# RWKV's three projections: both weight chunks split ahead, then all matmuls in one row

## The chip, the cores and the metric

The kernel runs on one core of one Trainium2 chip. The metric is device time in microseconds (us) of one launch. A core has a matrix engine (PE, with weight loads shown apart as PEld), a vector engine (DVE), a scalar engine (ACT), GpSimd (POOL) and SyncE (SP), which here issues the DMA transfers. Each engine runs its own instructions strictly in the order in which they stand in its program, and semaphores make it wait for others. PE's clock is granted by a throttle at one of two levels, 1.2 and 2.4 GHz; the profile shows a mean of them as a share of full speed.

## The reference

The function is a two-layer decoder trunk on x of 512 tokens by 1024 columns, all in fp32. In each layer two token mixers run on the same normalized input and are merged by gates; a feed-forward part and a small per-layer embedding part follow.

```
h   = rmsnorm(x)
q, k, v, rw, gate_a, gate_b = split(h @ w_in)
y_att = sliding_window_attention(rope(q), rope(k), v, sinks) @ w_o_att
y_rw  = rwkv7_time_mix(rw, ...) @ w_o_rw
x += rmsnorm((sigmoid(gate_a)*y_att + sigmoid(gate_b)*y_rw) @ w_out)
x += rmsnorm((gelu(conv(h2 @ w_up)[a]) * conv(h2 @ w_up)[b]) @ w_down)
x += rmsnorm(sigmoid(x @ w_ple_gate) * (p @ w_ple))
```

The change lies in rwkv7_time_mix. It takes r, k and v (1024 columns each, 16 heads of 64) from h, shifts each by one token, forms a decay from a low-rank product and runs a recurrence over the tokens, in which each head has a 64 x 64 state:

```
r, k, v = shifted(h @ w_r), shifted(h @ w_k), shifted(h @ w_v)
state = state*w_t + (state @ a_t) b_t^T + v_t k_t^T
y_t   = state @ r_t
```

The kernel computes the recurrence in eight chunks of 64 tokens, which needs for each chunk the products of the decayed a, r, b and k (the tiles AR, bk, A and AM) and the inverse of a unit triangular matrix (the tile Z).

## The kernel before, in words

**Matmuls in two parts.** A product in fp32 is made of three fp32r matmuls: the weight tile w (128 columns, 4 blocks of 128 rows, 256 KB) is loaded by one DMA on SP; ACT writes its rounded part wh (L125, called in load_w); DVE subtracts and writes the rest wl (L155). mm3 (L244 to L249) then issues three matmuls of 512 columns for each block of 128 rows: wh by the high part of the activations (L247), wh by their low part (L248), wl by the high part (L249). A projection of 1024 rows has two such chunks, 24 matmuls. Its chunk loads are called w_r.10 and w_r.11 below for column block j=5 of w_r (chunks 2j and 2j+1). The weight pool has, for class "m", two buffers for w, three for wh and three for wl; the sums stand in a PSUM tile pm (two buffers) or pf (one).

**The RWKV stage.** rwkv_prep (L581) prepares one column block j of 128 columns, which holds two heads; there are eight in a layer. It makes k by a projection and a shift (an ACT instruction and a DVE instruction, L366 to L368), the decay (thw, D, Di), kksq with a matmul of ones and its sums to DRAM (ssp), bk and the a-half of AR, then r by a projection and a shift, the r-half of AR, the 32 small matmuls A of 128 x 128, masked by DVE into AM, bkT by transposes, and v by a projection and a shift. rwkv_group (L737) takes two preparations as one group (four groups in a layer): rwkv_inverse (L674) solves the triangular system by 62 short DVE instructions on Z, stores and reloads Z through DRAM (zd), and finishes it with small matmuls of 32 x 32 on PE (t1 and z12, with ACT and DVE copies between them); then a scan over the eight chunks runs, a chain of matmuls of 64 x 64 (xs, sp) with ACT and DVE copies between them.

**What sets the order.** All is traced into one program, and a scheduler puts every instruction in an order on its engine by its priority, the place at which the program emitted it, and by what it waits for. Work of other parts, above all the projections for the gates (w_gb) and the attention output (w_oa), which stand later in the program, is put between the small matmuls where the scheduler sees an engine waiting. tc.high_priority(offset=60), which the change uses, lifts what is emitted within it by 60 places in that priority. The order is fixed when the program is built; on the chip no engine departs from it.

Of the kernel before, what the change touches and what calls it, by code (L numbers as in the profile page):

```python
# [19 lines left out]
P = 128  # L20
T = 512
DM = 1024
KT = DM // P
# [32 lines left out]
class Trunk:  # L56
# [525 lines left out]
    def rwkv_prep(self, l, j, gi, R, X2, DC, ssp, nd):  # L582
        nc, a, h, vv, dv, rp = self.nc, self.a, self.h, self.vv, self.dv, R.rp
        NP_ = 32
        c1 = slice(j, j + 1)
        Tm = R.T
        q = Ctx()

        def ch(t):
            return t.rearrange("p (c t) -> p c t", t=C)  # L590
        k = self.shift(self.proj(a["w_k"][l, j], h), "k", j, Tm("k"))
        wa2 = self.load_w(a["w_wa2"][l, j], 2, low=((slice(64, 128), slice(0, 1)), (slice(0, 64), slice(1, 2))))
        th, ta = Tm("thw"), Tm("tha")
        for i, (t, n) in enumerate(((th, "w0h"), (ta, "a0h"))):
# [30 lines left out]
            self.tt(bk[:, :, x, :], ch(us[x]), ch(Di), ALU.mult)  # L625
        self.ts(ta, ta, dv["ka1"][:, c1], dv["ka2"][:, c1])
        self.tt(k, k, ta, ALU.mult)
        r = self.shift(self.proj(a["w_r"][l, j], h), "r", j, Tm("r"))
        self.tt(rv, ch(r), ch(D), ALU.mult)
        self.stt(r, r, vv("r_k")[:, c1], k, ALU.mult, ALU.mult)  # L630

# [15 lines left out]
        for hf in range(2):  # L647
# [4 lines left out]
            t = rp.tile([P, 4, P], F32, name="bkT", tag="bkT", bufs=6)  # L652
            self.act(t, tp.rearrange("p (c x) -> p c x", c=4))
            q.bkT.append(t)
        v = self.shift(self.proj(a["w_v"][l, j], h), "v", j, Tm("v"))
        bon = self.PT("bonus")
        self.last_prep = nc.tensor.matmul(bon, self.blockones, r, start=True, stop=True).ins
        vp = self.PT("vT")
# [536 lines left out]
```

## Time and profile before

| | before |
|---|---|
| median of 3 runs | 2365.49 us (2357.16 to 2371.89) |
| the profiled execution | 2361.03 us, span 2359.2 us |
| mean granted PE clock | 0.976 |
| PE busy | 2230.6 us, 95% of the span, 14340 matmuls |
| PE weight loads busy | 1757.7 us, 75% |
| DVE busy | 1555.0 us, 66% |
| ACT busy | 1123.3 us, 48% |
| POOL busy | 26.5 us, 1% |

The profiled execution is 4.46 us below the median of the runs. The RWKV stage of layer 0 lies at about 220 to 640 us of the span, that of layer 1 at about 1385 to 1810 us. An instruction's row gives its start, its duration, its engine and line, its tiles as out<-in, the number of like instructions drawn together (x16), and in brackets how long the engine had been idle before it and what ended that. PE's durations overlap: a 512-column matmul is shown with 0.39 us, and the next starts 0.23 us after it.

### The profile page before, as it was taken

To read this page: it belongs to the slowest core of one execution; us is meant where nothing else is said; L and a number is where in the kernel's file an instruction comes from. 1 tells how busy PE (TensorE), PEld (TensorE's weight loads), DVE (VectorE), ACT (ScalarE), POOL (GpSimd) and SP (SyncE) were. 2 spreads that over 40 slices of the span, in tenths; PEclk is the share of its full clock that TensorE was granted. 3 is DMA by queue.
4 is the path that set the end of the run, shared out by engine and by line. 5 is a ranking of instruction groups with operands and counts; after the bars stand their busy time and mean duration, and the time that the engine had idled before them with its cause. 6 is when DMAs were issued, how large, how long until landed. Compare 5 with 4: busy or idle time off the path is not lost. (4 is left out here: it accounts for less than half of the span.)

```text
span 2359.2 us, 39516 instructions
## 1 busy us (share of the span) xinstructions
PE 2230.6 (95%) x14340; PEld 1757.7 (75%) x14340; DVE 1555.0 (66%) x3683; ACT 1123.3 (48%) x2450; POOL 26.5 (1%) x86
## 2 busy tenths in 40 slices
PE   7899999999999999999898999999999999999995
PEld 6666776667689788888795667766677887888895
DVE  6764589767566777733777647778566668776355
ACT  4466445544444544432445655545444445444332
POOL 1000000000000000000000000000000000000000
PEclk9999999989999999999999999999899999999998
DMA  4522333245571332342334233332356713333422
GB/s 146 163 79 94 108 90 86 79 123 169 176 250 35 123 99 94 94 119 87 99 115 145 88 110 95 90 91 83 107 162 198 239 58 104 98 95 102 121 72 81
DMA packets 206818, 269.39 MB, mean 114 GB/s; under 512 B 72096, under 2 KB 88992, under 8 KB 206624
## 3 DMA queue, kind: packets, MB, share of 16 engines
q1 hardware_dynamic: 206624, 266.88, 37.0%
q8 instruction: 113, 1.85, 0.3%
q14 instruction: 81, 0.66, 0.1%
HBM read 218.95 MB, written 42.47 MB: 111 GB/s over the span
## 5 line engine op out<-in xcount | busy, mean ns | idle before, releaser
L125 ACT ACTIVATE wh<-w 128x512 fp32r<-128x512 f32 (+1 forms) x590 | 353.1, 606 | 556.7 <-PE pm L248 176.8
L155 DVE TENSOR_TENSOR wl<-w,wh 128x512 fp32r<-128x512 f32 (+2 forms) x574 | 376.6, 662 | 263.4 <-ACT wh L125 255.6
L249 PE MATMUL pm<-hh,wl 128*128 128x512 f32 x1040 | 424.0, 408 | 9.4 <-DVE wl L155 9.2
L247 PE MATMUL pm<-hh,wh 128*128 128x512 f32 x1040 | 424.6, 408 | 2.8 <-DVE Z L696 1.1
L248 PE MATMUL pm<-hl,wh 128*128 128x512 f32 x1040 | 420.1, 404 | 0.1
L249 PEld LDWEIGHTS pm<-hh,wl 128*128 128x128 f32 x1040 | 198.0, 190 | 56.5 <-DVE wl L155 12.9
L247 PEld LDWEIGHTS pm<-hh,wh 128*128 128x128 f32 x1040 | 198.0, 190 | 49.4 <-issue 5.6
L247 PE MATMUL pf<-hh,wh 128*128 128x512 f32 x544 | 219.2, 403 | 16.2 <-ACT wh L125 10.4
L248 PEld LDWEIGHTS pm<-hl,wh 128*128 128x128 f32 x1040 | 197.6, 190 | 46.6 <-issue 6.5
L249 PE MATMUL pf<-hh,wl 128*128 128x512 f32 x544 | 216.8, 398 | 3.2 <-DVE wl L155 3.0
L248 PE MATMUL pf<-hl,wh 128*128 128x512 f32 x544 | 215.8, 397 | 0.0
L134 DVE SCALAR_TENSOR_TENSOR cv<-un,vec,cv 128x510 f32<-128x510 f32 (+1 forms) x176 | 131.0, 750 | 24.6 <-ACT cv L125 22.0
L247 PEld LDWEIGHTS pf<-hh,wh 128*128 128x128 f32 x544 | 102.5, 188 | 45.9 <-ACT wh L125 20.3
L249 PEld LDWEIGHTS pf<-hh,wl 128*128 128x128 f32 x544 | 102.4, 188 | 32.6 <-DVE wl L155 8.6
L248 PEld LDWEIGHTS pf<-hl,wh 128*128 128x128 f32 x544 | 102.6, 189 | 21.3 <-issue 1.8
L247 PE MATMUL pm<-uh,wh 128*128 128x512 f32 (+1 forms) x248 | 89.1, 359 | 3.6 <-ACT wh L125 3.6
L249 PE MATMUL pm<-uh,wl 128*128 128x512 f32 (+1 forms) x248 | 89.1, 360 | 0.0
L248 PE MATMUL pm<-ul,wh 128*128 128x512 f32 (+1 forms) x248 | 88.8, 359 | 0.0
L125 ACT ACTIVATE cv<-un,vec 128x512 f32<-128x512 f32 x88 | 71.3, 814 | 25.4 <-DVE un L128 25.4
L128 DVE TENSOR_TENSOR acc<-acc,sq 128x256 f32<-128x256 f32 (+1 forms) x114 | 50.1, 464 | 37.9 <-ACT sq L125 37.2
L530 DVE CUSTOM_DVE_ANT_0 sm<-scores,tmask 128x256 f32<-128x256 f32 (+1 forms) x128 | 43.5, 384 | 36.0 <-PE scores L117 36.0
L128 DVE TENSOR_TENSOR un<-pm,rs 128x512 f32<-128x512 f32 x56 | 38.5, 690 | 41.2 <-PE pm L249 41.1
(402 smaller groups left out, 4457.9 us busy)
## 6 DMA issues: line engine op xcount, KB each, us to landing
w<-in_w_up_dram SPq DMA_DIRECT2D x156, 256.0 KB
w<-in_w_dn_dram SPq DMA_DIRECT2D x80, 256.0 KB
w<-in_w_q_dram SPq DMA_DIRECT2D x32, 256.0 KB
w<-in_w_ga_dram SPq DMA_DIRECT2D x32, 256.0 KB
w<-in_w_k_dram SPq DMA_DIRECT2D x32, 256.0 KB
w<-in_w_r_dram SPq DMA_DIRECT2D x32, 256.0 KB
w<-in_w_v_dram SPq DMA_DIRECT2D x32, 256.0 KB
w<-in_w_gb_dram SPq DMA_DIRECT2D x32, 256.0 KB
```

What stands on the lines that cost most here:

```text
L125: return self.nc.scalar.activation(out=out, in_=in_, func=func, **kw)
L128: return self.nc.vector.tensor_tensor(out=out, in0=in0, in1=in1, op=op)
L134: return self.nc.vector.scalar_tensor_tensor(out=out, in0=in0, scalar=s, in1=in1, op0=op0, op1=op1)
L155: self.nc.vector.tensor_tensor(out=wl, in0=w, in1=wh.bitcast(F32), op=ALU.subtract)
L247: mm(ps, wh, ah, start=start, stop=False)
L248: mm(ps, wh, al, start=False, stop=False)
L249: return mm(ps, wl, ah, start=False, stop=stop).ins
L530: nc.vector.tensor_tensor_reduce(out=sm[i][:, par * 256:par * 256 + KW], in0=scs[par][:, x * 256:x * 256 + KW], in1=tm, scale=1.0, scalar= ...
```

## The change

The three calls of proj in rwkv_prep are replaced. proj loads and splits one chunk of four row blocks, issues its 12 matmuls, then does the same for the second chunk. The new function ahead loads and splits both chunks by the existing function whole, within high_priority(offset=60); the new function pr then takes one PSUM tile and issues all 24 matmuls. Loads, splits and matmuls are the same in number and size.

```diff
@@ -588,7 +588,16 @@
-        k = self.shift(self.proj(a["w_k"][l, j], h), "k", j, Tm("k"))
+        def ahead(name):
+            with self.tc.high_priority(offset=60):
+                return self.whole(a[name][l, j], P, "m")
+
+        def pr(ws):
+            ps = self.PM("m")
+            for i, w in enumerate(ws):
+                self.mm3(ps, w, h[i], i == 0, i == KT - 1)
+            return ps
+        k = self.shift(pr(ahead("w_k")), "k", j, Tm("k"))
...
-        r = self.shift(self.proj(a["w_r"][l, j], h), "r", j, Tm("r"))
+        r = self.shift(pr(ahead("w_r")), "r", j, Tm("r"))
...
-        v = self.shift(self.proj(a["w_v"][l, j], h), "v", j, Tm("v"))
+        v = self.shift(pr(ahead("w_v")), "v", j, Tm("v"))
```

In the order of the instructions the column blocks j=0 to 4 of each layer change by a few rows; j=5, 6 and 7 change much, on PE, ACT, DVE and SP. POOL's order stays. Lines below L591 are nine higher in the changed kernel (L715 becomes L724).

**The first place: DVE, column block j=5 of layer 0.** Before, wl_4615 is the first chunk of w_r (k_4563 is this block's k, Z the inverse of the group before, yo a later result of the group before that):

```order
L134 SCALAR_TENSOR_TENSOR AR_4589<-k_4563,nkk_571,D_4583 128x8x63
L696 TENSOR_TENSOR Z_3787<-Z_3787,Z_3788 128x14x5
L128 TENSOR_TENSOR v_4510<-bonus_4513,v_4510 128x512
L694 TENSOR_TENSOR Z_3788<-rin_3789,Z_3787 128x56
L131 TENSOR_SCALAR AR_4589<-k_4563,nkk_571 128x8
L128 TENSOR_TENSOR yo_3315<-yo_3315,bv_3313 128x512
L696 TENSOR_TENSOR Z_3787<-Z_3787,Z_3788 128x14x4
L128 TENSOR_TENSOR yo_3315<-yo_3315,g_3314 128x512
L694 TENSOR_TENSOR Z_3788<-rin_3789,Z_3787 128x45
L128 TENSOR_TENSOR Di_4584<-k_4563,Di_4584 128x512
L696 TENSOR_TENSOR Z_3787<-Z_3787,Z_3788 128x15x3
L155 TENSOR_TENSOR wl_4615<-w_4611,wh_4613 128x512
```

With the change both chunks of w_r (wl_4614 and wl_4620) stand here, ahead of the shift of this block's k:

```order
L128 TENSOR_TENSOR grt_3297<-gry_3295 128x16
L155 TENSOR_TENSOR wl_4614<-w_4610,wh_4612 128x512
L134 SCALAR_TENSOR_TENSOR grt_3297<-grt_3297,gvar_3284 128x16
L703 TENSOR_TENSOR Z_3788<-rin_3789,Z_3787 128x91
L134 SCALAR_TENSOR_TENSOR gry_3295<-grt_3297,gry_3295 128x16
L155 TENSOR_TENSOR wl_4620<-w_4616,wh_4618 128x512
```

The first split of w_r moved ten instructions of Z forward, and the second stands four rows behind it; the shift of k, which stood ahead of both, is now 12 rows behind the second. On SP the two loads of w_v for j=5 moved likewise, ahead of the small transfers of ssp and zd; on PE the 24 matmuls of this block's v moved ahead of its matmuls A.

**The second place: PE, the inverse of the third group (j=4 and 5) of layer 0.** t1 and z12 are the inverse's small matmuls, A those of j=7, pm_5659 the sum of v for j=7, pm_6306 one of w_gb. Before:

```order
L715 MATMUL t1_4837<-zT_4833,AM_4430 32x32
L117 MATMUL A_5617<-AR_5552,bk_5553 128x128
L117 MATMUL A_5618<-AR_5552,bk_5553 128x128
L724 MATMUL z12_4856<-Z_4750,t1_4834 32x32 x8
L117 MATMUL A_5617<-AR_5552,bk_5553 128x128
L724 MATMUL z12_4857<-Z_4750,t1_4834 32x32 x8
L117 MATMUL A_5618<-AR_5552,bk_5553 128x128
```

With the change:

```order
L724 MATMUL t1_4837<-zT_4833,AM_4430 32x32
L247 MATMUL pm_6306<-hh_109,wh_6327 128x512
L248 MATMUL pm_6306<-hl_110,wh_6327 128x512
L733 MATMUL z12_4856<-Z_4750,t1_4834 32x32 x8
L249 MATMUL pm_6306<-hh_109,wl_6329 128x512
L733 MATMUL z12_4857<-Z_4750,t1_4834 32x32 x8
L247 MATMUL pm_6306<-hh_111,wh_6327 128x512
```

The matmuls A of j=7 stand ahead of this inverse now, and 512-column matmuls of w_gb stand between its steps.

**The third place: PE, the inverse of the last group (j=6 and 7) of layer 0.** pf_6622 is a sum of w_oa. Before:

```order
L715 MATMUL t1_5800<-zT_5796,AM_5393 32x32
L247 MATMUL pf_6622<-hh_105,wh_6625 128x512
L248 MATMUL pf_6622<-hl_106,wh_6625 128x512
L724 MATMUL z12_5819<-Z_5713,t1_5797 32x32 x8
L249 MATMUL pf_6622<-hh_105,wl_6627 128x512
L724 MATMUL z12_5820<-Z_5713,t1_5797 32x32 x8
L247 MATMUL pf_6622<-hh_107,wh_6625 128x512
```

With the change:

```order
L724 MATMUL t1_5799<-zT_5796,AM_5392 32x32
L724 MATMUL t1_5800<-zT_5796,AM_5393 32x32
L733 MATMUL z12_5819<-Z_5713,t1_5797 32x32 x8
L733 MATMUL z12_5820<-Z_5713,t1_5797 32x32 x8
L724 MATMUL t1_5848<-zT_5845,AM_5615 32x32
L724 MATMUL t1_5849<-zT_5845,AM_5616 32x32
```

All matmuls of pf_6622 now stand ahead of this inverse, and none is left between its steps and those of the scan's first chunk. In layer 1 the inverse of the last group keeps 512-column matmuls of w_oa between its steps.

## Rows read from the trace of the kernel before

**Rows 1.** The page's first part: busy time of the engines, share of the span, number of instructions.

```profile
PE 2230.6 (95%) x14340; PEld 1757.7 (75%) x14340; DVE 1555.0 (66%) x3683; ACT 1123.3 (48%) x2450; POOL 26.5 (1%) x86
```

**Rows 2.** The page's costliest groups: line, engine, operation, out<-in, shapes, count, then busy time and mean ns of one, then the idle time of the engine just before them and what ended most of it.

```profile
L125 ACT ACTIVATE wh<-w 128x512 fp32r<-128x512 f32 (+1 forms) x590 | 353.1, 606 | 556.7 <-PE pm L248 176.8
L155 DVE TENSOR_TENSOR wl<-w,wh 128x512 fp32r<-128x512 f32 (+2 forms) x574 | 376.6, 662 | 263.4 <-ACT wh L125 255.6
L249 PE MATMUL pm<-hh,wl 128*128 128x512 f32 x1040 | 424.0, 408 | 9.4 <-DVE wl L155 9.2
L247 PE MATMUL pm<-hh,wh 128*128 128x512 f32 x1040 | 424.6, 408 | 2.8 <-DVE Z L696 1.1
```

**Rows 3.** Stretches of 40 us in the RWKV stage of layer 0: start and end, length, then busy time and number of instructions of PE, PEld, DVE, ACT and POOL, then the granted PE clock, the DMA engines' busy share and GB/s.

```profile
400.00:440.00 40.00, 35.91 (x403) 24.94 (x403) 26.26 (x67) 16.36 (x42) 1.22 (x4) 0.91 0.47 126
440.00:480.00 40.00, 39.23 (x352) 27.75 (x351) 38.08 (x109) 24.71 (x59) 0.53 (x1) 1.00 0.27 80
480.00:520.00 40.00, 36.26 (x356) 26.04 (x354) 21.80 (x52) 16.04 (x38) 1.22 (x4) 0.79 0.39 97
560.00:600.00 40.00, 39.82 (x497) 27.81 (x495) 20.60 (x49) 19.83 (x55) 1.22 (x4) 1.00 0.54 161
```

**Rows 4.** The same view and columns, layer 1.

```profile
1560.00:1600.00 40.00, 35.26 (x354) 24.70 (x352) 25.09 (x62) 17.15 (x39) 1.22 (x4) 0.87 0.38 97
1600.00:1640.00 40.00, 35.69 (x368) 24.53 (x367) 37.80 (x112) 22.52 (x61) 0.53 (x1) 0.96 0.26 81
1640.00:1680.00 40.00, 37.74 (x270) 28.22 (x269) 24.40 (x56) 18.21 (x36) 1.22 (x4) 0.80 0.35 92
1680.00:1720.00 40.00, 39.56 (x438) 27.55 (x438) 27.85 (x83) 20.26 (x59) 0.00 (x0) 0.90 0.43 130
```

**Rows 5.** PE's waits between 380 and 500 us: the waiting group, what it waited for, us in total, how many times, the longest.

```profile
PE pm L249 <- DVE wl L155: 3.6, 3, 1.7
PE A L117 <- DVE AR L128: 2.4, 1, 2.4
PE pm L247 <- DVE Z L696: 1.1, 1, 1.1
PE pm L597 <- ACT thw L125: 0.9, 1, 0.9
```

**Rows 6.** PE's waits between 1545 and 1690 us, the same columns.

```profile
PE A L117 <- DVE AR L128: 3.0, 2, 2.4
PE A L117 <- DVE AM L128: 2.4, 2, 1.9
PE pm L597 <- ACT thw L125: 2.1, 1, 2.1
PE pm L249 <- DVE wl L155: 1.4, 1, 1.4
...
PE pm L247 <- ACT wh L125: 0.6, 1, 0.6
```

**Rows 7.** PE in order of time, the projection of r for j=5 and the matmuls A behind it, layer 0.

```profile
402.12 0.50 PE L249 MATMUL pm<-hh,wl 128*128 128x512 f32 x1 [1.37 <-DVE wl L155]
402.46 0.40 PE L247 MATMUL pm<-hh,wh 128*128 128x512 f32 x1
402.70 0.39 PE L248 MATMUL pm<-hl,wh 128*128 128x512 f32 x1
...
410.16 1.20 PE L117 MATMUL A<-AR,bk 64*128 64x128 f32 x16 [2.38 <-DVE AR L128]
```

**Rows 8.** DVE in order of time in the same stretch: the splits of w_r.10 and w_r.11, and the shift of r.

```profile
401.38 0.68 DVE L155 TENSOR_TENSOR wl<-w,wh 128x512 fp32r<-128x512 f32 x1
...
404.48 0.68 DVE L155 TENSOR_TENSOR wl<-w,wh 128x512 fp32r<-128x512 f32 x1
...
408.54 0.75 DVE L134 SCALAR_TENSOR_TENSOR r<-pm,vec,r 128x511 f32<-128x511 f32 x1 [0.35 <-ACT r L125]
```

**Rows 9.** ACT in order of time: the first chunk of w_v for j=5, layer 0.

```profile
410.76 0.63 ACT L125 ACTIVATE wh<-w 128x512 fp32r<-128x512 f32 x1 [2.25 <-DMA w<-in_w_v_dram]
```

**Rows 10.** Shorter stretches, with the columns of rows 3: the third group's inverse and first scan steps of layer 0, the matmuls A of j=5 in layer 1, the third group's inverse and first scan steps of layer 1.

```profile
500.00:515.00 15.00, 15.00 (x166) 11.29 (x164) 7.13 (x17) 4.63 (x14) 0.00 (x0) 0.55 0.21 55
1580.00:1590.00 10.00, 10.00 (x120) 7.65 (x119) 2.41 (x5) 1.27 (x4) 0.00 (x0) 0.56 0.47 122
1667.00:1688.00 21.00, 20.93 (x193) 15.39 (x189) 7.25 (x20) 4.64 (x14) 0.00 (x0) 0.51 0.15 36
```

**Rows 11.** PE in order of time in the third group's inverse of layer 0.

```profile
501.84 1.06 PE L715 MATMUL t<-zT,AM 32*32 32x32 f32 x32
```

**Rows 12.** PE in order of time in the last group's inverse and first scan step of layer 0.

```profile
571.18 0.69 PE L715 MATMUL t<-zT,AM 32*32 32x32 f32 x32
571.80 0.50 PE L247 MATMUL pf<-hh,wh 128*128 128x512 f32 x1
572.14 0.40 PE L248 MATMUL pf<-hl,wh 128*128 128x512 f32 x1
572.47 0.69 PE L724 MATMUL z<-Z,t 32*32 32x32 f32 x16
...
579.96 0.40 PE L248 MATMUL pf<-hl,wh 128*128 128x512 f32 x1
580.28 0.45 PE L782 MATMUL sp<-X,bkT 128*64 128x64 f32 x8
```

**Rows 13.** DVE in order of time: the last step of that sum of w_oa, with the gate.

```profile
582.95 0.69 DVE L134 SCALAR_TENSOR_TENSOR ta<-ta,pf 128x512 f32<-128x512 f32 x1 [0.38 <-PE pf L249]
```

## The prediction

> **What bounds the kernel now.** I read the totals first. PE is busy for 2230.6 of 2359.2 us [rows 1], no other engine for more than 66%, so a change that only moves work can win two things: idle time of PE, 128.6 us in all, and time in which PE's clock is at the lower level. The groups say who ends PE's idle time where weight splits are concerned: all 1040 matmuls of L249 into pm waited 9.2 us for wl together, those of L247 2.8 us for anything [rows 2]. That is the first thing to see: the waits which the title of the change is about are worth about 9 us in 2361, spread over all parts of the kernel that use pm, not RWKV alone.
>
> The second look is at the stage, cut into stretches of 40 us. In layer 0 PE is short of busy time only where j=5 and j=7 are prepared, 35.91 and 36.26 us of 40, and DVE is nearly full in the stretch between, 38.08 [rows 3]. Layer 1 has the same picture, with 35.26, 35.69 and 37.74 us [rows 4]. The same rows carry the clock: 0.91, 0.79, 0.87, 0.96, 0.80 and 0.90. Its shortfall, (1 - clock) x 40, is 3.6 + 8.4 = 12.0 us in layer 0 and 5.2 + 1.6 + 8.0 + 4.0 = 18.8 us in layer 1. So the slow clock is worth more here than the idle time.
>
> The third look is at the waits by name [rows 5, 6] and, for the clock, at shorter stretches [rows 10]. The slow stretches at 500 and 1667 us have no idle time to speak of, 15.00 of 15.00 and 20.93 of 21.00 us busy, and 0.55 and 0.51 of the clock. What runs in them are the inverse's 32 x 32 products, A and the scan's 64 x 64 products with few 512-column matmuls between. The last group's inverse of layer 0 has the same small products with 512-column matmuls between them [rows 12], in a stretch at clock 1.00 [rows 3]. The same 32 products take 1.06 us in the one [rows 11] and 0.69 in the other [rows 12].
>
> **The change part by part.** Loads, splits and matmuls stay the same in number and size, so no busy time is added. Only order counts, and only j=5, 6 and 7 of each layer change theirs. Splits cost 0.68 us on DVE and wh 0.63 us on ACT [rows 8, 9].
>
> *Column block j=5.* PE waited 1.37 us for wl of w_r.10 and 2.38 us for AR [rows 7]; layer 1 has 1.4 and 2.4 and another 0.6 for wh of w_v, which came late [rows 6]; in layer 0 that load came late too (ACT idle for 2.25 us on it [rows 9]) behind the small transfers on SP. All of these go: the splits of w_r stand earlier, v's loads stand ahead of those transfers, and 23 of v's matmuls, 23 x 0.23 = 5.3 us, now run while r is shifted and AR formed, against the 2.38 us needed. Gone are 3.75 and 4.4 us. What is late next is k: its shift stands behind two splits, 2 x 0.69 = 1.4 us, and the whole chain of D, Di, bk and AR behind it, on a DVE that is 95% full. The cover is r's 24 matmuls; a bound below is nothing, above 2.8 us if v's two splits ahead of bk count as well. I take 1.4, as only the first pair stands ahead of k. Gain 2.35 + 3.0 = 5.35 us (from 1.0 + 1.6 to 3.75 + 4.4).
>
> *j=6.* In layer 0 it had no wait of size, and it now gets its 512-column matmuls of k in a row while two more splits stand ahead of Z's steps on DVE; its next k load stands behind ssp and zd on SP. I charge two waits of the size of the late wh, 0.6 [rows 6], less some cover: 0.9 us (from 0 to 1.4). In layer 1 the waits for AR, 0.6 of the 3.0, and for AM, 2.4 [rows 6], get v and k matmuls as cover; I take half of 3.0, 1.5 (from 0 to 3.0). Together a gain of 0.6 us.
>
> *j=7, waits.* In layer 0 they are 0.9 for thw, 1.1 for Z and 3.6 - 1.37 = 2.2 for wl, of which 1.67 is here: 3.7 us [rows 5]. The thw chain is untouched. The wl wait goes, but v's splits now stand ahead of AM's masks on DVE, and A runs earlier, when less has been done for it. I take 0.9 won (from -1.0 to 3.7). In layer 1 the 2.1 us for thw stay [rows 6]: 0.
>
> *Third group, clock.* A of j=7 now runs before the inverse, and w_gb's 512-column matmuls stand between the inverse's and the scan's steps, the mix that ran at 1.00 in the last group. The shortfall is 0.45 x 15 = 6.8 us in layer 0 and 0.49 x 21 = 10.3 us in layer 1 [rows 10]. The small products wait for copies in part, so not all of it comes back: 6 and 8 us (from 0 to 6.8 and 10.3). At j=5 of layer 1 another 0.44 x 10 = 4.4 us is short [rows 10]; A there stays a block of small products, I take 1 (from 0 to 4.4).
>
> *Last group of layer 0.* Its cover is gone: from 571.80 to 579.96 us 14 matmuls of pf lay in seven places between the steps [rows 12], at 0.33 us from start to start 14 x 0.33 = 4.6 us, which now stand ahead and leave as many us of bare waiting. On DVE the last step of that sum, 0.69 us [rows 13], now stands ahead of the transpose on which the first small product waits. So 5.3 us of idle time, and I expect the clock to fall in or after it, for some 6 us at half, 3 us. Cost 8.3 us (from 4.6 to 12).
>
> The loads' place on SP and wh's on ACT cost nothing by themselves: ACT is 16 to 25 us of 40 busy [rows 3], and if that cover failed the late-load wait of 0.6 us [rows 6] a block would come back.
>
> Sum: 5.35 + 0.6 + 0.9 + 6 + 8 + 1 - 8.3 = 13.6 us won. Of the profiled execution, 2361.0 - 13.6 = 2347.4; the median of the three runs shown is 4.5 higher than that execution, so the forecast is 2365.5 - 13.6 = **2352 us**. With the terms' bounds not all at one end it reaches from 2344 to 2362.
>
> **The page and the row on the clock.** Rows 10 show the low level in stretches without idle time. The Trainium skill, TensorE: Matmul & The Clock Gate, section "HAM oscillation — how this bites in real kernels", puts a falling clock down to waits of PE between bursts of matmuls. By that rule exchanging A for w_gb in a busy stretch returns nothing, the clock terms 6, 8 and 1 are zero, and the last group of layer 0, which does get waits, is the only place where the clock could change. The rows of the slow stretches speak against it, so I keep the terms; it is the third rival.
>
> **Rivals.** *The clock comes back everywhere (chance 0.17).* If the full shortfall of both layers, 12.0 + 18.8 us, went, with 5.35 of waits at j=5, 3.0 - 0.9 = 2.1 at j=6, 0.9 at j=7, and the last group at its 5.3 us of idle time alone: 30.8 + 8.35 - 5.3 = 33.9 us, 2332 us. For it speaks that the stretch at 560 us holds 1.00 with the same small products; against it that A at j=5 keeps its own block.
>
> *Slower: the splits ahead hold up Z (0.17).* At j=5 and 6 DVE is 38.08 and 37.80 us of 40 busy and Z's 62 steps run there one behind another, each behind what is put between. Six splits a block, 6 x 0.69 = 4.1 us, now stand ahead of Z's end, AM and the k chain. It decides once PE's filler, which is finite, has run out before the inverse can start: every us of delay then is a us of PE. The last group of layer 0 shows that point reached. Were it so for j=5 and 6 in both layers, 4 x 4.1 = 16.5 us come in with the 8.3, against 8.2 us of the removed waits at j=5 and no clock won: 16.6 us slower, 2382 us. Against it: the splits were on the same DVE before, only later, and all had to be done by the same matmuls.
>
> *The clock is not a matter of the filler (0.16).* With the clock terms at nothing the waits won are 6.85 and the last group costs 5.3 to 8.3: 1.5 us faster to 1.5 slower, 2364 to 2367 us. For it: 1580 to 1590 us has 10.00 of 10.00 busy and 0.56 [rows 10], so busy time alone does not hold the clock, and I do not know that w_gb does.
>
> The forecast keeps 0.50.
>
> **How the numbers follow.** The range reaches from 2332, the first rival, to 2374, half way to the slower one's time; below and above it about a tenth each is left. A measurement of this kernel can tell about 1% from no change, 24 us: under 2342 or over 2389. Faster by that much are most of the first rival and the forecast's best corner, 0.13 + 0.03 = 0.16; slower the upper end of the second rival, 0.05; the rest, 0.79, is within.
>
> **What would show it.** In the changed profile, PE's waits for wl at j=5 and for AR behind r are gone in both layers; the third group's inverses are at a clock above 0.9 in both layers; the last group of layer 0 shows PE idle for about 5 us between t1, z12 and xs, with the clock falling there; k's shift and thw at j=6 and 7 end PE's new waits, none over 2 us. The forecast is wrong if the third group's stretches stay at half clock with w_gb in them, if PE's idle time before the inverses of both layers grows by more than the 8 us removed at j=5, or if the last group of layer 1 loses its cover as well.

## The result and the profile after

| | before | with the change |
|---|---|---|
| median | 2363.85 us (2357.16 to 2371.89, 4 runs) | 2338.68 us (2334.68 to 2339.89, 4 runs) |
| ratio | | 0.9889, 95% interval 0.9855 to 0.9923 |
| profiled execution | 2361.03 us | 2339.11 us |
| span, mean PE clock | 2359.2 us, 0.976 | 2337.1 us, 0.984 |

The change makes the kernel 25 us faster by the medians, 22.1 us by the spans of the two profiled executions. The forecast was 13.6 us. The ratios here and below are the record's estimates over all runs; they can differ by up to 0.002 from the quotient of the two medians.

The page's first part, to be read against [rows 1]:

```profile
PE 2211.3 (95%) x14340; PEld 1742.5 (75%) x14340; DVE 1550.4 (66%) x3683; ACT 1123.8 (48%) x2450; POOL 27.5 (1%) x86
```

PE has the same 14340 matmuls and is busy 2230.6 - 2211.3 = 19.3 us less. Its idle time fell from 128.6 to 2337.1 - 2211.3 = 125.8 us, by 2.8 us. So seven eighths of what was won are matmuls that run faster, and one eighth is waiting that went. The costliest groups say the same of the waits for splits, against [rows 2]: L249 into pm had waited 9.2 us for wl, and now waits 6.4.

```profile
L247 PE MATMUL pm<-hh,wh 128*128 128x512 f32 x1040 | 425.2, 409 | 2.2 <-ACT wh L125 1.8
L249 PE MATMUL pm<-hh,wl 128*128 128x512 f32 x1040 | 420.7, 404 | 6.4 <-DVE wl L155 6.4
```

The stage in each layer, cut from PE's first small matmul of the first inverse to the last normalization of the merge. The columns are those of [rows 3]. Before:

```profile
342.10:718.40 376.30, 363.10 (x3240) 267.47 (x3239) 262.75 (x662) 186.70 (x441) 4.72 (x14) 0.96 0.48 144
1508.10:1889.90 381.80, 367.16 (x3240) 272.05 (x3239) 263.52 (x662) 186.58 (x441) 4.72 (x14) 0.95 0.47 142
```

With the change:

```profile
342.70:711.10 368.40, 354.98 (x3239) 261.90 (x3238) 260.73 (x662) 187.37 (x441) 4.72 (x14) 0.98 0.48 147
1499.30:1864.30 365.00, 354.06 (x3239) 259.32 (x3238) 261.45 (x662) 186.16 (x441) 4.73 (x14) 1.00 0.49 148
```

Layer 0's stage is 7.9 us shorter, layer 1's 16.8, together 24.7; the remaining 2.6 us were lost outside these cuts, where at most a few rows of the order change. Length less busy time is PE's idle time: 13.2 us before and 13.4 after in layer 0, 14.6 and 10.9 in layer 1. All of layer 0's gain and 13.1 of layer 1's 16.8 us are busy time, with the clock at 0.98 and 1.00 in place of 0.96 and 0.95.

PE's waits between 380 and 500 us, which answer to [rows 5]:

```profile
PE pm L606 <- ACT thw L125: 1.2, 2, 0.8
PE pm L249 <- DVE wl L155: 1.0, 1, 1.0
PE ss L621 <- ACT kksq L125: 0.9, 2, 0.4
PE pm L247 <- ACT wh L125: 0.6, 1, 0.6
```

And between 1545 and 1690 us in layer 1, which answer to [rows 6]:

```profile
PE pm L606 <- ACT thw L125: 2.6, 2, 1.8
PE pm L249 <- DVE wl L155: 1.8, 1, 1.8
PE pm L247 <- ACT wh L125: 1.2, 2, 0.6
```

The waits for AR, 2.4 us in layer 0 and 3.0 in layer 1, are gone, and so is the wl wait of r at j=5. New ones, for thw, kksq and wh, end the places that came next, and in layer 1 a wait of 1.8 us for wl that was not there before, at 1642.59 us.

The slow stretches of [rows 10] and the last group of layer 0, with the columns of [rows 3]: first the third group of layer 0, then its last group, then the third group of layer 1.

```profile
498.00:518.00 20.00, 20.00 (x297) 13.72 (x295) 7.85 (x23) 9.88 (x27) 0.00 (x0) 1.00 0.45 124
564.00:582.00 18.00, 15.20 (x242) 11.31 (x243) 5.75 (x16) 7.31 (x22) 0.00 (x0) 0.62 0.43 138
1656.00:1676.00 20.00, 20.00 (x299) 13.51 (x299) 8.72 (x25) 9.60 (x28) 0.00 (x0) 1.00 0.53 159
```

The third groups, at 0.55 and 0.51 before, are at 1.00. The inverse of the last group of layer 0, at 1.00 before, is the one that got worse. PE there in order of time, to be set against [rows 12]:

```profile
564.27 0.69 PE L724 MATMUL t<-zT,AM 32*32 32x32 f32 x32 [2.10 <-DVE zT L719]
565.40 1.09 PE L733 MATMUL z<-Z,t 32*32 32x32 f32 x32 [0.43 <-ACT t L125]
567.17 0.85 PE L724 MATMUL t<-zT,AM 32*32 32x32 f32 x32 [0.68 <-DVE zT L719]
568.43 1.73 PE L733 MATMUL z<-Z,t 32*32 32x32 f32 x32 [0.41 <-ACT t L125]
...
571.36 0.69 PE L784 MATMUL xs<-scr,Z 64*64 64x64 f32 x8 [0.58 <-ACT scr L125]
572.47 0.69 PE L791 MATMUL sp<-X,bkT 128*64 128x64 f32 x8 [0.42 <-DVE X L786]
```

The gaps add up to 2.10 + 0.43 + 0.68 + 0.41 + 0.58 + 0.42 = 4.6 us, and the same products slow down on the way, t from 0.69 to 0.85 us and z from 1.09 to 1.73.

### The profile page after: what moved, and what is told of

Read it like the earlier page. It is cut to its first block, busy times and chain, and to the rows that moved or that the text cites. A ratio compares the mean times of both kernels' runs of the same rounds, so it can differ in the third digit from the quotient of the medians.

```text
span 2337.1 us, 39500 instructions
## 1 busy us (share of the span) xinstructions
PE 2211.3 (95%) x14340; PEld 1742.5 (75%) x14340; DVE 1550.4 (66%) x3683; ACT 1123.8 (48%) x2450; POOL 27.5 (1%) x86
## 5 line engine op out<-in xcount | busy, mean ns | idle before, releaser
L249 PE MATMUL pm<-hh,wl 128*128 128x512 f32 x1040 | 420.7, 404 | 6.4 <-DVE wl L155 6.4
L249 PEld LDWEIGHTS pm<-hh,wl 128*128 128x128 f32 x1040 | 196.6, 189 | 50.4 <-DVE wl L155 7.9
L249 PE MATMUL pf<-hh,wl 128*128 128x512 f32 x544 | 217.4, 400 | 3.3 <-DVE wl L155 3.1
L247 PEld LDWEIGHTS pf<-hh,wh 128*128 128x128 f32 x544 | 102.8, 189 | 46.2 <-ACT wh L125 18.8
L249 PEld LDWEIGHTS pf<-hh,wl 128*128 128x128 f32 x544 | 102.7, 189 | 32.6 <-DVE wl L155 8.9
L249 PE MATMUL pm<-uh,wl 128*128 128x512 f32 (+1 forms) x248 | 89.1, 360 | 0.0
```

The costliest lines, as they stand in the source:

```text
L247: mm(ps, wh, ah, start=start, stop=False)
L249: return mm(ps, wl, ah, start=False, stop=stop).ins
```

## The experiments

Two theories stood at the start. Mine: the raised priority moves the matmuls so that 512-column matmuls come to lie in the third group's inverse, and this decides the clock there. The rival of the first runs: it is the 24 matmuls in a row, or each projection's early splits bring a share.

**Whole projections without the priority.** The with statement goes, all else stays:

```diff
         def ahead(name):
-            with self.tc.high_priority(offset=60):
-                return self.whole(a[name][l, j], P, "m")
+            return self.whole(a[name][l, j], P, "m")
```

> The loads and splits of both chunks stand together and the 24 matmuls in a row, but without the raised priority. In the order of the instructions the third group's inverse has 4 and 5 512-column matmuls between its steps and 15 and 12 matmuls A, as before the change. Theory (the raised priority carries the gain, by what it moves into the third group): the time of before, 2362 us within 6, third group at clock 0.5 to 0.6. Rival (24 matmuls in a row carry it): the changed kernel's time, 2339 us.

Measured: 2358.15 us against 2358.48 before, ratio 0.9994 (0.9979 to 1.001). The third groups stay slow:

```profile
498.00:514.00 16.00, 16.00 (x183) 12.24 (x179) 7.67 (x19) 4.78 (x14) 0.00 (x0) 0.57 0.27 72
1663.00:1681.00 18.00, 17.93 (x159) 12.81 (x160) 7.15 (x19) 4.77 (x16) 0.00 (x0) 0.53 0.15 39
```

So 24 matmuls in a row, with both splits together but not raised, are worth nothing by themselves.

**The priority with the matmuls in two chunks.**

```diff
         def ahead(name):
-            with self.tc.high_priority(offset=60):
-                return self.whole(a[name][l, j], P, "m")
-
-        def pr(ws):
+            return a[name][l, j]
+
+        def pr(src):
             ps = self.PM("m")
-            for i, w in enumerate(ws):
-                self.mm3(ps, w, h[i], i == 0, i == KT - 1)
+            for k0 in (0, 4):
+                with self.tc.high_priority(offset=60):
+                    wh, wl = self.load_w(src[:, k0:k0 + 4, :], 4, P, "m")
+                for k in range(4):
+                    self.mm3(ps, (wh[:, k], wl[:, k]), h[k0 + k], k0 + k == 0, k0 + k == KT - 1)
```

> Each chunk's load and split is raised by 60, the matmuls come in two times 12 as before. Third group with 17 and 18 512-column matmuls and no A, last group of layer 0 with none, as in the changed kernel. Theory (priority carries it): 2339 us within 5. Rival (24 in a row): 2362 us.

Measured: 2337.64 us, ratio 0.9904 (0.988 to 0.9927). The priority carries the whole gain.

**One projection at a time.** The other two use proj as before; here the edit for w_r alone.

```diff
-        k = self.shift(pr(ahead("w_k")), "k", j, Tm("k"))
+        k = self.shift(self.proj(a["w_k"][l, j], h), "k", j, Tm("k"))
...
-        v = self.shift(pr(ahead("w_v")), "v", j, Tm("v"))
+        v = self.shift(self.proj(a["w_v"][l, j], h), "v", j, Tm("v"))
```

> Only w_r's two chunks are split ahead; w_k and w_v as before. The third groups get 18 512-column matmuls, and the last group of layer 0 keeps 17. Theory (filler in the inverse decides clock and idle time): no half clock in either, so the changed kernel's gain and about 8 us more from the last group of layer 0 (4.6 us idle, and about half of 13.7 us at half clock less what the copies take), while v's late load and the AR wait at j=5 return in part, 2 us in each layer: 2334 us, 2328 to 2340. Rival (each projection's early splits carry a third of the gain): 2355 us.

> Only w_k's two chunks are split ahead. The third groups have 4 and 5 512-column matmuls and 15 and 12 A, as before. Theory: 2362 us within 6, third groups at clock 0.5 to 0.6. Rival (each projection a third): 2355 us.

> Only w_v's two chunks are split ahead. The third groups keep 11 and 13 matmuls A with 7 512-column matmuls. Theory: the wl wait of r at j=5 stays, the AR wait and v's late load go (2.4 to 3.0 us in each layer), the third group's clock stays under 0.8 in both layers: 2354 us, 2348 to 2360. Rival (A in the inverse does not matter, filler of any number does): third groups at 1.00 and 2340 us.

Measured: w_r alone 2331.9 us, ratio 0.9883 (0.9859 to 0.9907); w_k alone 2361.15 us, 1.0005 (0.9984 to 1.0026); w_v alone 2361.28 us, 1.000 (0.9978 to 1.0022). The first two came as expected. w_v missed: 2354 us were expected by the AR wait that was to go, and it wins nothing. In its trace the AR wait of 2.38 us at j=5 is still there in both layers, so early loads of v without an earlier r do not give A its cover. Its third group in layer 0, with 7 512-column matmuls and 11 A in the inverse (22 by the trace, which shows each A twice), runs at half clock without a gap:

```profile
503.00:527.00 24.00, 23.96 (x263) 17.29 (x259) 8.16 (x19) 6.86 (x21) 0.00 (x0) 0.57 0.27 73
```

**Two calls of 48.** w_r is split ahead at j=5 alone, everything else as before:

```diff
-        r = self.shift(self.proj(a["w_r"][l, j], h), "r", j, Tm("r"))
+        r = self.shift(pr(ahead("w_r")) if j == 5 else self.proj(a["w_r"][l, j], h), "r", j, Tm("r"))
```

> w_r's two chunks are split ahead at j=5 alone, in both layers: two calls of 48. In the order of the instructions all inverses have the same number of 512-column matmuls as with w_r ahead at all j. Theory (the lever is that r of j=5 comes earlier, so that all later work of j=6 and 7 moves up by as much): as with w_r ahead everywhere, 2332 us within 5. Rival (each column block adds its share): at most a third of the gain, 2350 us.

Measured: 2328.57 us (2326.32 to 2329.62), ratio 0.9860 (0.9828 to 0.9892), the fastest of all. PE's idle time in its two stages is 359.0 - 352.36 = 6.6 and 363.4 - 352.09 = 11.3 us, and the clock is at 1.00 throughout:

```profile
343.20:702.20 359.00, 352.36 (x3239) 257.96 (x3238) 259.75 (x662) 186.27 (x441) 4.72 (x14) 1.00 0.49 151
1489.70:1853.10 363.40, 352.09 (x3240) 258.49 (x3239) 262.06 (x662) 186.29 (x441) 4.72 (x14) 1.00 0.49 149
```

So r of j=5 alone is enough for the whole gain. Its split stands behind Z's steps before the change, and with it earlier all that follows on PE, through j=7's A, moves ahead of the third group's inverse.

**All but those two calls.**

```diff
-        r = self.shift(pr(ahead("w_r")), "r", j, Tm("r"))
+        r = self.shift(self.proj(a["w_r"][l, j], h) if j == 5 else pr(ahead("w_r")), "r", j, Tm("r"))
```

> The changed kernel without the early splits of w_r at j=5 alone (two calls of 48). In the order of the instructions the third group of layer 0 has 7 512-column matmuls and 11 A in its inverse, that of layer 1 has 13 and no A; the last group of layer 0 has 17. Theory (the clock follows that count): half clock stays in the third group of layer 0, goes in that of layer 1; the wl wait of 1.4 us at j=5 is back in both layers: 2347 us, 2341 to 2353. Rival (r at j=5 is the whole change): 2360 us; rival (each projection and block its share): 2340 us.

Measured: 2353.25 us (2344.12 to 2365.66), ratio 0.9973 (0.9948 to 0.9998). Three quarters of the gain are gone, and a quarter, 6.6 us, is left without r of j=5. The time lies just above the range that I gave, between it and the 2360 us of the rival. The third group of layer 0 kept half clock in part, 6.8 us, that of layer 1 lost it, as counted; but layer 1's second group, with 11 512-column matmuls and 4 A (8 by the trace), was slow in this execution, 18.2 us at half clock.

**w_r alone in layer 0, all three in layer 1.**

> w_r alone ahead in layer 0, all three in layer 1. Theory: layer 0 as with w_r alone, which keeps the last group's cover, 5.6 us less than the changed kernel by the start of the embedding part; layer 1 as in the changed kernel: 2331 us, 2326 to 2336. Rival (the layers are not independent, since the schedule moves on): 2339 us.

Measured: 2333.79 us, ratio 0.9879 (0.9839 to 0.9918), as expected. It can't be told from w_r alone in both layers, and the rival's 2339 us lies above all its runs.

**More work as filler.** The rest of the question was whether the last group of layer 0 is slow because its cover ran out. Redundant matmuls were put into the changed kernel's inverse there, n at each of four steps. In the first kernel n was 3 and each matmul was also tied to its place in the program; in the second n was 5 and in the third 3, without the tie. The lines stand behind t1 and again behind z12, and both are passed twice:

```diff
+            if l == 0 and grp == 3:
+                jk = self.PT("jk")
+                for i in range(n):
+                    nc.tensor.matmul(jk, self.h[i][0][:, 0:P], self.h[i][0], start=True, stop=True)
```

> The changed kernel with 12 more 512-column matmuls, whose sums nothing reads, three after each of the four steps t1, z12, t1, z12 of the last group of layer 0; nothing is left out. At full clock they are 12 x 0.23 = 2.8 us of added work on PE. Theory (that inverse lost clock and idle time because no 512-column matmuls lay in it): the stretch of some 20 us from the inverse's start is back at 1.00, PE's gaps there fall below 0.5 us each, and the kernel is not slower in spite of the added work: 2335 us, 2331 to 2340. Rival (the chain of copies sets that stretch, the clock is not a matter of what lies between): 2.8 us slower or the same, clock there still 0.5 to 0.6.

Measured: 2347.7 us, ratio 0.994 (0.9917 to 0.9963), a miss that does not decide: the tied matmuls drew the whole inverse forward on PE, past the work that had stood ahead of it, and PE waited for Z in one piece:

```profile
565.00 1.07 PE L724 MATMUL t<-zT,AM 32*32 32x32 f32 x32 [12.60 <-DVE zT L719]
```

Behind that wait the inverse ran at half clock without a gap, though the added matmuls lay in it; so the clock came out as the rival had said, but behind a wait that neither side had foreseen:

```profile
565.00:575.30 10.30, 10.30 (x141) 7.05 (x141) 1.29 (x3) 3.00 (x8) 0.00 (x0) 0.50 0.22 60
```

Without the tie the scheduler uses the added matmuls as filler ahead of the inverse, and w_oa's own come to lie in it:

> The changed kernel with 20 more 512-column matmuls (five at each of the four steps of the inverse of the last group of layer 0, not tied to their place; sums that nothing reads, nothing left out). The scheduler puts them ahead of that inverse as filler, and 17 of w_oa's own matmuls come to lie between the inverse's steps, where the changed kernel has none. Added work 20 x 0.23 = 4.6 us. Theory (the last group of layer 0 loses idle time and clock because filler ran out): idle time of some 3 us and the 13.7 us at half clock there go, worth 3 + 0.43 x 13.7 = 9 us, so the kernel with more work is faster: 2334 us, 2329 to 2339. Rival (work is work; clock and waits of that place are set by the small products): 2343 us, half clock stays there.

> The same with 12 added matmuls, three a step: 5 of w_oa's matmuls come to lie in that inverse, all in its first half. Added work 2.8 us. Theory: the idle time there falls to about half, the clock stays at half level for most of it (5 of 17 as in the third groups of the kernel before, which had 4 and 5 beside A): 2338 to 2342 us. Rival (any filler holds the clock): 2334 us.

Measured: 20 added, 2333.92 us, ratio 0.990 (0.9876 to 0.9924); 12 added, 2334.94 us, 0.9908 (0.9885 to 0.993). The place itself, first with 20 added and then with 12:

```profile
561.00:579.00 18.00, 18.00 (x274) 12.30 (x274) 7.16 (x18) 8.10 (x24) 0.00 (x0) 1.00 0.57 183
```

```profile
563.00:581.00 18.00, 16.29 (x254) 11.55 (x254) 6.10 (x16) 7.30 (x22) 0.00 (x0) 0.72 0.52 166
```

The added matmuls themselves ran some 25 us and more earlier, from 525 to 536 us; what lies in the inverse is w_oa's. With 17 of these 512-column matmuls in the inverse PE is busy 18.00 of 18.00 us at full clock; with 5, idle for 1.7 us and at 0.72; with none, in the changed kernel, idle for 2.8 of these 18 us and at 0.62. Idle time and filler change together here, so these three do not tell which of them the clock goes by. Twenty more matmuls, 4.6 us of work, left the kernel no slower by its median than the changed one, which the rival had excluded; that it is faster, 2334 against 2339, is not shown, for the two sets of runs overlap. With 12 the clock came out as I had said, at half for 10 us of it, and the time as the rival had, 2334.94 us, so these times do not tell the two apart. The clock in the rows, 0.72, goes against the rival: 5 did not hold it.

**The clock in the same order.** The profiled execution with 20 added matmuls holds one more thing. From the second group of layer 1 its order is that of the changed kernel, yet the clock was at half for most of 21 us there. First this execution, then the changed kernel's at the same place:

```profile
1572.00:1593.00 21.00, 20.47 (x212) 13.85 (x209) 5.92 (x17) 6.41 (x20) 0.00 (x0) 0.51 0.35 97
```

```profile
1575.00:1596.00 21.00, 19.23 (x291) 12.98 (x291) 12.17 (x35) 12.40 (x35) 0.00 (x0) 1.00 0.43 124
```

So the order does not settle the clock alone. Twelve of these kernels (before, after and all the others but the one with tied matmuls) have eight inverses each. For each inverse I counted the 512-column matmuls that lie between its first small matmul and the scan's first sp, and the half clock in the trace from 2 us before its start to 22 us after. Of 59 inverses with 14 to 23 such matmuls, two had any half clock, 3.4 us each. All 12 with 0 to 7 had some, 3.4 to 19.6 us. Of 25 with 10 to 13, 15 had none and the others up to 19.2 us. The tied kernel, which is left out, is an exception: 18 lie in its last group's inverse of layer 0, with 14.4 us at half clock behind the wait of 12.6 us.

The firmest part of this are the third groups. In the seven kernels where they have 17 or 18 512-column matmuls and no A, none of the 14 had any half clock; in the three where they have 4 or 5 and 24 to 30 A by the trace, all six had 13.7 to 18.8 us, and none of the 20 had idle time in the inverse. Whether it is the 512-column matmuls that were there or the A that were not was not tried: of the 12 inverses with 7 or fewer, nine hold A, and the other three, all of the last group of layer 0, hold idle time of 1.5 to 2.5 us. So the count goes with the clock, but a cause apart from A and from waits is not shown.

## Why the prediction came out as it did

The median, 2338.68 us, lies in the forecast's outer range, 2332 to 2374, but below the narrower one from the terms' bounds, 2344 to 2362, and in the part under 2342 that had been given a chance of 0.16. It is 6.7 us from the first rival's time and 13.3 from the forecast's own. What was forecast of the mechanism came, and one term was far too small. Of the signs named ahead, all came but one: k's shift ends no new wait of PE of size.

**What bounds the kernel.** It held that the clock is worth more than the waits, and that was so, by more than it said: 19.3 of 22.1 us.

**j=5.** 5.35 us were forecast from the waits for wl, AR and wh, with 1.4 us left in each layer. Gone are the waits for wl and AR in each layer; what is left of size ahead of the second inverse is 0.4 us for kksq in layer 0, and 0.5 for kksq and 0.6 for wh in layer 1. That step was right in kind, and its cost of 1.4 us a layer was set too high. DVE ran the two splits at 392.30 and 393.23 us, nine us before where the first had stood [rows 8]:

```profile
392.30 0.68 DVE L155 TENSOR_TENSOR wl<-w,wh 128x512 fp32r<-128x512 f32 x1
...
393.23 0.68 DVE L155 TENSOR_TENSOR wl<-w,wh 128x512 fp32r<-128x512 f32 x1
```

Which of the three projections does it was not told apart in the forecast: w_r alone.

**j=6 and j=7, waits.** 0.6 and 0.9 us were forecast. Layer 1's waits for AR and AM at j=6 are gone almost wholly, but new ones for thw, wh, kksq and wl took their place. In layer 0 the wait for wl at j=7 was to go and shrank from 1.67 to 1.0 us. PE's idle time of both stages together fell by 27.84 - 24.36 = 3.5 us, against 6.85 - 5.3 = 1.55 forecast, the last group's idle time included.

**The last group of layer 0.** 8.3 us forecast, 5.3 of idle time and 3 of clock. The trace shows 4.6 us of gaps and 13.7 us at half clock. To price both, the stage of layer 0 is set against that of w_r alone, which keeps the cover:

```profile
345.30:705.60 360.30, 352.28 (x3240) 258.08 (x3239) 259.88 (x662) 186.18 (x441) 4.73 (x14) 1.00 0.50 150
```

The difference is 368.4 - 360.3 = 8.1 us, 13.4 - 8.0 = 5.4 of idle time and 355.0 - 352.3 = 2.7 of busy time. By this comparison of two single executions the term was right. In part that is luck: the half clock lasted 13.7 us and not the 6 that were expected, and each of these us cost less than the 0.5 that was reckoned.

**The clock.** This is the term that was mis-sized. 6 + 8 + 1 = 15 us were set down. With the last group's cost of 8.1 us added back, layer 0's stage won 16.0 us where the steps without that group gave 8.35, and layer 1 won 16.8 where they gave 13.5. Of this, PE's busy time is 8.1 + 2.7 = 10.8 in layer 0 and 13.1 in layer 1, together 23.9 us where 15 stood. I had counted back most of the two third groups, a quarter of the 4.4 us at j=5 in layer 1, and nothing of the other short slow stretches, at j=5 and early in j=7 of layer 0 and at j=6 of layer 1 [rows 3, 4], nor of one at 636 us of layer 0. These short stretches before, three of layer 0 and two of layer 1, with the columns of [rows 3]:

```profile
408.00:424.00 16.00, 13.76 (x175) 10.34 (x176) 7.79 (x14) 3.64 (x8) 0.31 (x1) 0.79 0.52 134
484.00:492.00 8.00, 6.33 (x18) 4.17 (x19) 5.56 (x12) 4.95 (x10) 1.22 (x4) 0.79 0.41 90
634.00:642.00 8.00, 6.03 (x19) 4.53 (x19) 2.67 (x5) 3.02 (x5) 0.00 (x0) 0.79 0.77 255
1576.00:1592.00 16.00, 15.16 (x180) 11.57 (x180) 6.24 (x12) 3.13 (x7) 0.08 (x1) 0.68 0.45 112
1634.00:1646.00 12.00, 9.81 (x45) 7.86 (x46) 9.34 (x31) 3.45 (x6) 0.00 (x0) 0.72 0.25 66
```

In the trace after the change these are gone in layer 0, and in layer 1 all but 3.4 us. The stages up to the last inverse of layer 0 and to j=7 of layer 1, after the change:

```profile
342.70:560.00 217.30, 211.22 (x2176) 147.99 (x2176) 176.24 (x493) 122.54 (x298) 4.42 (x13) 1.00 0.40 115
1499.30:1640.00 140.70, 134.45 (x1426) 92.34 (x1426) 118.01 (x326) 83.94 (x206) 2.29 (x6) 1.00 0.33 96
```

The gaps that stood ahead of several of them are gone too; whether each went with its gap was not tried by itself. The price of a slow stretch can be read from the pair of executions with the same order above: from the first t1 of layer 1's second inverse to that of its third the one took 1660.19 - 1569.64 = 90.6 us, the other 1656.29 - 1573.04 = 83.3, for 20.5 us more at half clock, so 0.36 us were lost in each, not the 0.43 that was reckoned ahead of the added matmuls. An estimate by this price: the third groups' 13.7 and 20.5 us at half clock were worth 12 us, near the 6 + 8 set down, and the short stretches, some 27 us at half clock less after the change, were worth 10, where 1 stood.

**The row on the clock.** The forecast set the Trainium skill's account of a falling clock, TensorE: Matmul & The Clock Gate, section "HAM oscillation — how this bites in real kernels", waits of PE between bursts, against a row at half clock without idle time, and kept the row. The runs bear the row out: 23.96 of 24.00 us busy at 0.57, and 20.47 of 21.00 at 0.51. Nor did a wait stand ahead of the third group's fall in layer 0 of the kernel before:

```profile
490.00:499.90 9.90, 9.86 (x103) 7.90 (x103) 5.74 (x10) 3.28 (x7) 0.00 (x0) 1.00 0.31 64
499.90:513.60 13.70, 13.70 (x146) 10.22 (x146) 6.16 (x15) 4.46 (x13) 0.00 (x0) 0.50 0.22 60
```

Other places show waits ahead of a fall: 2.38 us for AR, ended at 410.16 us [rows 7], in the first of the short stretches above, and 12.60 us in the kernel with tied matmuls. Without the clock terms the forecast would have been 2364 to 2367 us, 25 us and more above the median measured.

**The rivals.** Clock everywhere, 2332 us: layer 1 came out so, layer 0 would have but for the last group, and w_r at j=5 alone reached it, 2328.57 us. Slower by splits ahead of Z: did not happen; Z's chain ends no wait of size except in the last group. The clock no matter of filler: its time, 2364 to 2367 us, lies above all four runs, and the third groups went to 1.00 without idle time before or after; but more filler came with fewer A, and with 10 to 13 the order does not decide.

## What to carry to other kernels

When a stage is bound by one engine and its clock moves, read the busy time at a constant number of instructions first: what a reordering gives can lie there and not in the waits that it was made for. A raised priority moves more than the instructions inside it; try it on each place by itself, for here two calls of 48 were enough for the whole gain, and with the other 46 added the kernel was 10 us slower than with those two alone, 2338.68 against 2328.57 us in separate sets of runs that do not overlap. Filler is finite: a place that is covered earlier is paid for at the last one, so look where the scheduler's reserve runs out.

## What the runs showed of the hardware

PE's clock was at its lower level in stretches in which PE had no idle time, 15.00 of 15.00 us busy at 0.55 [rows 10], while it ran 32 x 32, 64 x 64 and 128-column matmuls with few 512-column ones. In layer 0 it fell there behind 9.9 us at 1.00 that were busy for 9.86. With 17 and 18 512-column matmuls in place of A among the same small ones the third groups stood at 1.00, 20.00 of 20.00 us busy. After a wait of 12.60 us the lower level lasted on for 10.3 us of unbroken work with 512-column matmuls in it, at 0.50. And one order of instructions was run at either level in two executions, 1.00 and 0.51, for 21 us.
